# Gate chunks written out by quarters, and two blocks of experts taken out of the sorted lists, in a two-layer kernel on one core

## The chip, the cores and the metric

The kernel runs on one core of one Trainium2 chip. The metric is the time of one execution on the device, in microseconds (us). TensorE (PE) multiplies, VectorE (DVE) and ScalarE (ACT) do elementwise work, GpSimd (POOL) issues the indirect gathers, and SyncE (SP) issues plain loads. ACT also issues DMAs: its stores sit in the same in-order stream as its arithmetic.

## The reference

256 tokens of width 2048 go through two layers in float32. The part that matters here is the expert mixture at the end of the first layer: 16384 experts, 8 heads, 16 experts chosen for each head and token.

```python
q = (xt @ w_pq).reshape(T, PEER_HEADS, 2, PEER_HALF)
s1 = einsum('thd,hkd->thk', q[:, :, 0], sub_k1); s2 = einsum('thd,hkd->thk', q[:, :, 1], sub_k2)
v1, i1 = top_k(s1, 16); v2, i2 = top_k(s2, 16)
cand = (v1[..., :, None] + v2[..., None, :]).reshape(T, 8, 256)
cidx = (i1[..., :, None] * 128 + i2[..., None, :]).reshape(T, 8, 256)
sc, sel = top_k(cand, 16); eidx = take_along_axis(cidx, sel, -1); gates = softmax(sc)
act = gelu(einsum('cd,ced->ce', xc, u_emb[ic]))          # ic, gc: experts and gates of a token
out = einsum('ce,ced->cd', gc * act, v_emb[ic])
```

## The kernel before

**Precision.** Each weight tile is split into a high and a low part (`whi` on ACT, line 123; `wlo` on DVE, line 124), and `mm3` makes three matmuls of 128 x 512 from them (lines 134 to 136). A weight tile `raw` of 128 x 2048 comes by one DMA of 1 MB; `halves` makes two `whi` and two `wlo` of 128 x 1024 from it. There are 3 buffers of `raw` and 4 each of `whi` and `wlo`. One `whi` feeds 12 matmuls.

**The expert mixture.** It has two phases. In the U phase (loop over `n` in 32), PE multiplies all 16384 rows of `u_emb` by the tokens, ACT applies gelu (`act`, line 783), PE transposes (`tp`, line 790), ACT copies (`actT`, line 792) and ACT issues two stores into the DRAM table `AG` (line 794). Below that stream, at low priority, a second stream routes the tokens: top 16, then the gate matrix, then lists of the experts in use.

**Gate chunks.** The dense gate matrix (16384 experts x 256 tokens) is built in four chunks of 64 tokens. For each token PE multiplies two one-hot matrices (`sc`, line 667), ACT copies one half (`gh`, line 672), and DVE adds the other into `gsb` (line 673), a single buffer of 128 x 128 x 64. At the end of a chunk ACT issues two stores of `gsb` to `AG`, 2 MB each, in runs of 256 bytes (line 676), and DVE takes the maximum over the chunk's tokens in one instruction (lines 678 and 681).

**Lists and the V phase.** From those maxima the kernel sorts the experts into blocks of 128: `NA` blocks used by both halves of the tokens, `NB` by the first half alone, `NC` by the second. In the V phase POOL gathers, for each block, 128 rows of `v_emb` (into `raw` or `vraw`, line 130) and their gates and activations from `AG` (`vag`, line 130); `gated` multiplies these (`vh`, `vhh`, `vhl`) and `vblock` adds the block's product into eight PSUM banks: 24 matmuls for an `A` block, 12 for the others. If experts did not fit into the lists, a loop over all 128 blocks (`more > 0`) would finish them.

**Order.** The framework's scheduler lays out one static in-order instruction list for each engine from priorities and a timeline of its own. `prompt` lifts a few instructions of the routing stream to the U phase's priority.

Of the kernel before, what the change touches and what calls it, by code (L numbers as in the profile page):

```python
# [12 lines left out]
F32 = mybir.dt.float32  # L13
# [5 lines left out]
ALU = mybir.AluOpType  # L19
AX = mybir.AxisListType  # L20

P = 128
# [24 lines left out]
NR = _o  # L47


NA, NB, NC = 42, 29, 30  # L50
CAPA, CAP0, CAP1 = NA * 128, (NA + NB) * 128, (NA + NB + NC) * 128
NL = NA + NB + NC
NOWHERE = 127 * 128


@with_exitstack
def tile_kernel(ctx: ExitStack, tc: tile.TileContext, A, out):
    nc = tc.nc
    V, S, G, TE = nc.vector, nc.scalar, nc.gpsimd, nc.tensor

    def pool(name, bufs=1, space=None, stack=ctx):
        kw = {"space": space} if space is not None else {}
        return stack.enter_context(tc.tile_pool(name=name, bufs=bufs, **kw))
# [8 lines left out]
    def bank(name="bk"):  # L72
        tg, nb = {"lin": ("lin", 3), "tp": ("tp", 2), "sc": ("sc", 2), "z": ("sc", 2)}.get(name, ("x", 1))
        return pp.tile([P, 512], F32, tag=tg, name=name, bufs=nb)
# [29 lines left out]
    def wtile(src, step=2048, rows=None, raw=None):  # L104


        if raw is None:
            raw = wp.tile([P, 2048], F32, tag="raw", name="raw", bufs=3)
        if rows is not None:
            gather(raw, src, rows)  # L110
        else:
            for c in range(0, 2048, step):
                nc.sync.dma_start(raw[:, c:c + step], src[:, c:c + step])
        return halves(raw, min(step, 1024))

    def halves(raw, step):
        hi, lo = [], []
        for e in range(2):
            h = wp.tile([P, 1024], F32R, tag="whi", name="whi", bufs=WB)
            l = wp.tile([P, 1024], F32R, tag="wlo", name="wlo", bufs=WB)  # L120
            for c in range(0, 1024, step):
                r, q = raw[:, e * 1024 + c:e * 1024 + c + step], slice(c, c + step)
                S.activation(h[:, q], r, AF.Copy)  # L123
                V.tensor_sub(l[:, q], r, h[:, q].bitcast(F32))  # L124
            hi += [h[:, 0:512], h[:, 512:1024]]
            lo += [l[:, 0:512], l[:, 512:1024]]
        return hi, lo

    def gather(dst, src, rows):
        G.indirect_dma_start(out=dst, out_offset=None, in_=src,  # L130
                             in_offset=bass.IndirectOffsetOnAxis(ap=rows, axis=0))

    def mm3(ps, xh, xl, wh, wl, start, stop):
        TE.matmul(ps, lhsT=xh, rhs=wh, start=start, stop=False)  # L134
        TE.matmul(ps, lhsT=xh, rhs=wl, start=False, stop=False)  # L135
        TE.matmul(ps, lhsT=xl, rhs=wh, start=False, stop=stop)  # L136
# [224 lines left out]
    for c in range(2):  # L361
# [7 lines left out]
        for j in range(0, 4, 2):  # L369
# [9 lines left out]
            for jj in range(2):  # L379
                xh, xl = yl(4 * c + j + jj)  # L380
                split(y[:, jj, :], xh, xl, vcol("g_lru", 4 * c + j + jj))
                for tt in range(2):
# [4 lines left out]
                        axis=AX.X, op=ALU.add)  # L387
# [84 lines left out]
    for c in range(2):  # L472
        ps = linear(WIN, 5 + c, xt, range(4))
        qsb = []
        for tt in range(2):
            q = ap_.tile([P, 8, 64], F32, tag="qsb", name="qsb")
# [49 lines left out]
    AG = dp.tile([129 * P, 512], F32, tag="ag", name="ag")  # L526
    AGv = AG.rearrange("(i p) (e a t) -> p i e a t", p=P, e=2, a=2)
# [22 lines left out]
    for n in range(4):  # L550
        ps = linear(A["w_pq"], n, x1t, range(4))
        qs = []
        for tt in range(2):
            q = rq.tile([P, 512], F32, tag="rq", name="rq", bufs=2)
# [22 lines left out]
    @contextmanager  # L577
    def prompt():

        low[0] = tc.cur_priority  # L580
        tc.cur_priority = low0
        yield
        tc.cur_priority = low[0]
# [9 lines left out]
    for tt in range(2):  # L593
# [23 lines left out]
        for half, op, c in ((0, ALU.logical_shift_right, 4), (1, ALU.bitwise_and, 15)):  # L617
# [5 lines left out]
            for h in range(8):  # L623
# [4 lines left out]
                                op=ALU.mult)  # L628
# [15 lines left out]
    gp = pool("gates", 1, stack=r3p)  # L644


    used = rp.tile([P, 2, P], F32, tag="used", name="used")
# [3 lines left out]
    for c in range(4):  # L651
        gsb = gp.tile([P, P, 64], F32, tag="gsb", name="gsb", bufs=1)
        for t0 in range(0, 64, 4):
            t = 64 * c + t0
            io = iota.unsqueeze(1).to_broadcast([P, 4, P])
            oh = gp.tile([P, 4, P], F32R, tag="oh2", name="oh2", bufs=2)
            V.tensor_tensor(oh, io, i2T[:, t:t + 4].unsqueeze(2).to_broadcast([P, 4, P]), op=ALU.is_equal)
            o1 = gp.tile([P, 4, P], F32, tag="oh1", name="oh1", bufs=2)
            V.tensor_tensor(o1, io, i1T[:, t:t + 4].unsqueeze(2).to_broadcast([P, 4, P]), op=ALU.is_equal)
            og = gp.tile([P, 4, 2, P], F32R, tag="og", name="og", bufs=2)  # L660
            V.tensor_tensor(og[:, :, 1, :], o1, gT[:, t:t + 4].unsqueeze(2).to_broadcast([P, 4, P]), op=ALU.mult)
            for k0 in range(0, 4, 2):
                ps = bank("sc")
                for k in range(k0, k0 + 2):
                    with prompt():
                        S.activation(og[:, k, 0, :], o1[:, k, :], AF.Copy, scale=gTh[:, t + k:t + k + 1])
                        TE.matmul(ps[:, (k - k0) * T:(k - k0 + 1) * T], lhsT=oh[:, k, :],
                                  rhs=og[:, k].rearrange("p a b -> p (a b)"), start=True, stop=True)
                pv = ps.rearrange("p (k m i) -> p m i k", k=2, m=2)
                gh = gp.tile([P, P, 2], F32, tag="gh", name="gh", bufs=2)  # L670
                with prompt():
                    S.activation(gh, pv[:, 0], AF.Copy)
                    V.tensor_tensor(gsb[:, :, t0 + k0:t0 + k0 + 2], gh, pv[:, 1], op=ALU.add)
        h, t0 = c // 2, c % 2 * 64
        for e in range(0, P, 64):
            S.dma_start(AGv[:, 1 + e:65 + e, h, 1, t0:t0 + 64], gsb[:, e:e + 64, :])
        if t0 == 0:
            V.tensor_reduce(used[:, h, :], gsb, axis=AX.X, op=ALU.max)
        else:
            um = gp.tile([P, P], F32, tag="um", name="um")  # L680
            V.tensor_reduce(um, gsb, axis=AX.X, op=ALU.max)
            V.tensor_tensor(used[:, h, :], used[:, h, :], um, op=ALU.max)
    r3p.close()

# [12 lines left out]
    def kt_(name, n=1, dt=F32, bufs=1):  # L697
        return kp.tile([P, n, P], dt, tag=name, name=name, bufs=bufs)

    V.tensor_scalar(used, used, 0.0, None, op0=ALU.is_gt)  # L700
    m3 = kt_("m3", 3)
    V.tensor_tensor(m3[:, 0, :], used[:, 0, :], used[:, 1, :], op=ALU.mult)
    V.tensor_tensor(m3[:, 1:3, :], used, m3[:, 0:1, :].to_broadcast([P, 2, P]), op=ALU.subtract)
# [17 lines left out]
    for i, cap in enumerate((CAPA, CAP0, CAP1)):  # L721
        V.scalar_tensor_tensor(m3[:, i, :], rk[:, i, :], float(cap), m3[:, i, :], op0=ALU.is_lt, op1=ALU.mult)
    V.scalar_tensor_tensor(rk, rk, float(NOWHERE), m3, op0=ALU.subtract, op1=ALU.mult)
    place = kt_("place")
    V.tensor_tensor(place[:, 0, :], rk[:, 0, :], rk[:, 1, :], op=ALU.add)
    V.scalar_tensor_tensor(place[:, 0, :], rk[:, 2, :], float(NOWHERE), place[:, 0, :], op0=ALU.add, op1=ALU.add)
    pli, ti = kt_("pli", 1, I32), kt_("ti", 2, I32)
# [73 lines left out]
    vp = pool("vph", 2, stack=v1)  # L801
# [15 lines left out]
    def tiles_of(b):  # L817
        return (0, 1) if b < NA else (0,) if b < NA + NB else (1,)

    def gated(ag, n):  # L820

        h = vp.tile([P, 4, P], F32, tag="vh", name="vh", bufs=1)[:, 0:n]
        av = ag[:, 0:n * 256].rearrange("p (n a t) -> p n a t", a=2, t=P)
        V.tensor_tensor(h, av[:, :, 0], av[:, :, 1], op=ALU.mult)
        hh = vp.tile([P, 4, P], F32R, tag="vhh", name="vhh", bufs=4)[:, 0:n]
        S.activation(hh, h, AF.Copy)
        hl = vp.tile([P, 4, P], F32R, tag="vhl", name="vhl", bufs=4)[:, 0:n]
        V.tensor_tensor(hl, h, hh.bitcast(F32), op=ALU.subtract)
        return hh, hl

    got = {}
# [24 lines left out]
    def vblock(b, vh, vl, cs, stop=False):  # L856
        for c in cs:
            for tt in tiles_of(b):
                hh, hl = got[b][tt]
                mm3(acc[c][tt], hh, hl, vh[c], vl[c], fresh[tt], stop)  # L860
        for tt in tiles_of(b):
            fresh[tt] = False

    last = []
    for i, b in enumerate(order):
# [6 lines left out]
        vh, vl = wtile(VE, rows=idv[:, b:b + 1], raw=raw)  # L872
# [6 lines left out]
    with tc.If(more > 0):  # L879
        with tc.For_i(0, P, 1) as k:  # L880
            ag = vp.tile([P, 1024], F32, tag="vag", name="vag", bufs=3)
# [6 lines left out]
            hh, hl = gated(ag, 2)  # L888
            raw = wp.tile([P, 2048], F32, tag="raw", name="raw", bufs=3)
            nc.sync.dma_start(raw, VE[bass.ds(k * P, P), :])  # L890
            for c in range(4):
                r = raw[:, c * 512:(c + 1) * 512]
                vh = vp.tile([P, 512], F32R, tag="fh", name="fh", bufs=1)
                S.activation(vh, r, AF.Copy)
                vl = vp.tile([P, 512], F32R, tag="fl", name="fl", bufs=1)
                V.tensor_sub(vl, r, vh.bitcast(F32))
                for tt in range(2):
# [5 lines left out]
                    op=ALU.mult)  # L903
    ssp, ssq = small([P, 2, 4], "ssx"), small([P, 2, 4], "ssx")
    y1t = St(stp, 16, "y1t")
    for c in range(4):
        for i, (b, vh, vl) in enumerate(last):
            vblock(b, vh, vl, (c,), i == 1)
        resid(c, acc[c], None)
        tsplit(lambda tt, j: xs[:, tt, j * P:(j + 1) * P], y1t, 4 * c, 4, lambda j: gfm[:, j:j + 1])  # L910
# [95 lines left out]
    for h0 in (0, 4):  # L1006
        for tt in range(2):
            s = mq.tile([P, 4, T], F32, tag="s2", name="s2", bufs=2)
            for j in range(2):
# [3 lines left out]
                for hh in range(2):  # L1013
                    h = h0 + 2 * j + hh
# [80 lines left out]
    for h0 in (0, 4):  # L1095
        for tt in range(2):
# [4 lines left out]
            for e in range(2):  # L1101
                ps = bank("sc")
                b = slice(64 * e, 64 * e + 64)
                for j in range(2):
                    h = h0 + 2 * j + e
# [172 lines left out]
```

## Time and profile before

| | |
|---|---|
| median of 3 runs | 3051.96 us (3048.44 to 3052.6) |
| the profiled execution, its own time | 3049.11 us |
| its span from first to last instruction | 3047.3 us |
| PE busy | 2970.9 us, 97% |
| DVE / ACT / POOL busy | 66% / 52% / 9% |
| mean granted TensorE clock | 0.990 |
| U phase and routing | about 450 to 1259 us |
| four chunk ends | at 697.5, 828.9, 960.1 and 1087.1 us |
| V phase | about 1271 to 1667 us |

PE is busy nearly throughout, so what a change can win or lose shows as PE idle time, as the number of PE's matmuls, or as matmuls at the lower clock.

### The profile page before, as it was taken

To read this page: it belongs to the slowest core of one execution; us is meant where nothing else is said; L and a number is where in the kernel's file an instruction comes from. 1 tells how busy PE (TensorE), PEld (TensorE's weight loads), DVE (VectorE), ACT (ScalarE), POOL (GpSimd) and SP (SyncE) were. 2 spreads that over 40 slices of the span, in tenths; PEclk is the share of its full clock that TensorE was granted. 3 is DMA by queue.
4 is the path that set the end of the run, shared out by engine and by line. 5 is a ranking of instruction groups with operands and counts; after the bars stand their busy time and mean duration, and the time that the engine had idled before them with its cause. 6 is when DMAs were issued, how large, how long until landed. Compare 5 with 4: busy or idle time off the path is not lost. (4 is left out here: it accounts for less than half of the span.)

```text
span 3047.3 us, 36250 instructions
## 1 busy us (share of the span) xinstructions
PE 2970.9 (97%) x13729; PEld 2443.6 (80%) x13729; DVE 2002.0 (66%) x2944; ACT 1576.9 (52%) x2221; POOL 271.0 (9%) x232
## 2 busy tenths in 40 slices
PE   9999999998988999899999999999999999999999
PEld 7887888887877778678887788778888888888887
DVE  6885789877766769467777756664655454445454
ACT  6754545565655645455565555544444444344443
POOL 0000000000000000477662000000000000000000
PEclk9999999999999999999999999999999999999999
DMA  6442546656567575688886454554655555555554
GB/s 231 155 174 98 180 166 210 215 196 219 189 205 217 181 232 184 226 327 325 333 322 250 173 183 169 205 179 169 242 193 187 194 185 188 193 193 194 190 190 159
DMA packets 197168, 626.26 MB, mean 206 GB/s; under 512 B 82688, under 2 KB 116096, under 8 KB 129664
## 3 DMA queue, kind: packets, MB, share of 16 engines
q1 hardware_dynamic: 73728, 460.55, 42.8%
q0 software_dynamic: 20784, 124.79, 11.1%
q10 hardware_dynamic: 102480, 38.58, 4.8%
q8 instruction: 108, 1.77, 0.2%
q14 instruction: 68, 0.56, 0.1%
HBM read 583.77 MB, written 40.11 MB: 205 GB/s over the span
## 5 line engine op out<-in xcount | busy, mean ns | idle before, releaser
L124 DVE TENSOR_TENSOR wlo<-raw,whi 128x1024 fp32r<-128x1024 f32 (+1 forms) x972 | 1181.4, 1221 | 772.5 <-ACT whi L123 759.8
L123 ACT ACTIVATE whi<-raw 128x1024 fp32r<-128x1024 f32 (+1 forms) x972 | 1023.4, 1057 | 1087.0 <-PE lin L136 901.6
L134 PE MATMUL lin<-whi,x1th 128*128 128x512 f32 x1152 | 451.5, 399 | 25.4 <-ACT whi L123 25.4
L135 PE MATMUL lin<-wlo,x1th 128*128 128x512 f32 x1152 | 457.9, 397 | 6.2 <-DVE wlo L124 6.2
L136 PE MATMUL lin<-whi,x1tl 128*128 128x512 f32 x1152 | 457.1, 397 | 0.0
L134 PEld LDWEIGHTS lin<-whi,x1th 128*128 128x128 f32 x1152 | 219.6, 191 | 70.0 <-ACT whi L123 27.7
L136 PE MATMUL lin<-whi,x3tl 128*128 128x512 f32 x704 | 274.9, 391 | 0.0
L135 PE MATMUL lin<-wlo,x3th 128*128 128x512 f32 x704 | 274.2, 389 | 0.0
L134 PE MATMUL lin<-whi,x3th 128*128 128x512 f32 x704 | 269.5, 390 | 0.0
L135 PEld LDWEIGHTS lin<-wlo,x1th 128*128 128x128 f32 x1152 | 220.4, 191 | 51.3 <-DVE wlo L124 8.5
L136 PEld LDWEIGHTS lin<-whi,x1tl 128*128 128x128 f32 x1152 | 220.1, 191 | 43.5
L135 PE MATMUL lin<-wlo,y1th 128*128 128x512 f32 x512 | 200.7, 393 | 0.8 <-DVE wlo L124 0.8
L134 PE MATMUL lin<-whi,y1th 128*128 128x512 f32 x512 | 199.4, 395 | 1.7 <-ACT y1th L159 1.2
L136 PE MATMUL lin<-whi,y1tl 128*128 128x512 f32 x512 | 198.5, 393 | 0.8 <-DVE y1tl L160 0.8
L135 PEld LDWEIGHTS lin<-wlo,x3th 128*128 128x128 f32 x704 | 132.2, 188 | 27.3
L136 PEld LDWEIGHTS lin<-whi,x3tl 128*128 128x128 f32 x704 | 132.2, 188 | 27.1
L134 PEld LDWEIGHTS lin<-whi,x3th 128*128 128x128 f32 x704 | 132.2, 188 | 26.9
L130 POOL DMA_INDIRECT vag<-ag,idg x102 | 134.2, 1315 | 53.7 <-issue 26.5
L136 PE MATMUL lin<-whi,at 128*128 128x512 f32 x352 | 137.2, 390 | 0.0
L135 PE MATMUL lin<-wlo,at 128*128 128x512 f32 x352 | 137.0, 389 | 0.0
L134 PE MATMUL lin<-whi,at 128*128 128x512 f32 x352 | 135.5, 389 | 0.0
L134 PEld LDWEIGHTS lin<-whi,y1th 128*128 128x128 f32 x512 | 96.2, 188 | 22.4 <-ACT y1th L159 1.8
(440 smaller groups left out, 4750.1 us busy)
## 6 DMA issues: line engine op xcount, KB each, us to landing
raw<-in_u_dram SPq DMA_DIRECT2D x128, 1024.0 KB, 4.8
raw<-in_w_in_dram SPq DMA_DIRECT2D x91, 1024.0 KB, 4.8
raw<-in_w_gu_dram SPq DMA_DIRECT2D x88, 1024.0 KB, 4.8
raw<-in_w_dn_dram SPq DMA_DIRECT2D x44, 1024.0 KB, 4.7
raw<-in_w_out_dram SPq DMA_DIRECT2D x16, 1024.0 KB, 4.8
raw<-in_w_pq_dram SPq DMA_DIRECT2D x16, 1024.0 KB, 4.8
ag<-actT ACTq DMA_DIRECT2D x64, 256.0 KB, 3.0
ag<-gsb ACTq DMA_DIRECT2D x8, 2048.0 KB, 15.5
```

The lines of the kernel that those rows point to most:

```text
L123: S.activation(h[:, q], r, AF.Copy)
L124: V.tensor_sub(l[:, q], r, h[:, q].bitcast(F32))
L130: G.indirect_dma_start(out=dst, out_offset=None, in_=src, in_offset=bass.IndirectOffsetOnAxis(ap=rows, axis=0))
L134: TE.matmul(ps, lhsT=xh, rhs=wh, start=start, stop=False)
L135: TE.matmul(ps, lhsT=xh, rhs=wl, start=False, stop=False)
L136: TE.matmul(ps, lhsT=xl, rhs=wh, start=False, stop=stop)
```

## The change

Each chunk's last addition, its stores and its maximum are cut into four pieces of 32 experts: four additions (line 683 after), four stores of 1 MB (line 684) and four maxima (line 685). The number of 256-byte runs stays the same. Besides, `NB` and `NC` go down by one each, the first two blocks of 128 experts are marked as not in use for the lists (line 708), and the V phase starts with these two whole blocks, for both halves of the tokens: their `vag` and `v_emb` rows come by plain loads from SP, not by gathers.

```diff
-NA, NB, NC = 42, 29, 30
+NA, NB, NC = 42, 28, 29
+ND = 2
...
+                last = t0 + k0 == 62
                 with prompt():
                     S.activation(gh, pv[:, 0], AF.Copy)
-                    V.tensor_tensor(gsb[:, :, t0 + k0:t0 + k0 + 2], gh, pv[:, 1], op=ALU.add)
+                    if not last:
+                        V.tensor_tensor(gsb[:, :, t0 + k0:t0 + k0 + 2], gh, pv[:, 1], op=ALU.add)
         h, t0 = c // 2, c % 2 * 64
-        for e in range(0, P, 64):
-            S.dma_start(AGv[:, 1 + e:65 + e, h, 1, t0:t0 + 64], gsb[:, e:e + 64, :])
+        um = gp.tile([P, P], F32, tag="um", name="um")
+        for e in range(0, P, 32):
+            q = slice(e, e + 32)
+            V.tensor_tensor(gsb[:, q, 62:64], gh[:, q], pv[:, 1, q], op=ALU.add)
+            S.dma_start(AGv[:, 1 + e:33 + e, h, 1, t0:t0 + 64], gsb[:, q, :])
+            V.tensor_reduce(um[:, q], gsb[:, q, :], axis=AX.X, op=ALU.max)
         if t0 == 0:
-            V.tensor_reduce(used[:, h, :], gsb, axis=AX.X, op=ALU.max)
+            V.tensor_copy(used[:, h, :], um)
         else:
-            um = gp.tile([P, P], F32, tag="um", name="um")
-            V.tensor_reduce(um, gsb, axis=AX.X, op=ALU.max)
             V.tensor_tensor(used[:, h, :], used[:, h, :], um, op=ALU.max)
...
     V.tensor_scalar(used, used, 0.0, None, op0=ALU.is_gt)
+    V.memset(used[:, :, 0:ND], 0.0)
...
+    ag = vp.tile([P, 1024], F32, tag="vag", name="vag", bufs=3)
+    for k in range(ND):
+        nc.sync.dma_start(ag[:, k * 512:(k + 1) * 512], AG[(k + 1) * P:(k + 2) * P, :])
+    hh, hl = gated(ag, 2 * ND)
+    for k in range(ND):
+        got[-1 - k] = [(hh[:, 2 * k + tt], hl[:, 2 * k + tt]) for tt in range(2)]
+        vh, vl = wtile(A["v"][k])
+        vblock(-1 - k, vh, vl, range(4))
```

The scheduler lays the rest out anew. Three places follow, as the built programs list them; the numbers behind the names are buffers, which differ between the programs.

ACT at the end of the second chunk, before: the stores of `gsb` stand on either side of two stores of `actT`, and a `whi` follows each.

```order
L676 DMA ag_2894<-gsb_4469 128x64x64
L794 DMA ag_2894<-actT_8349 128x4x128 x2
L123 ACTIVATE whi_8470<-raw_8468 128x1024
L676 DMA ag_2894<-gsb_4469 128x64x64
L123 ACTIVATE whi_8474<-raw_8468 128x1024
L672 ACTIVATE gh_4847<-sc_4842 128x256
L666 ACTIVATE og_4876<-oh1_4874,gTh_2910 128x128 x4
L123 ACTIVATE whi_8525<-raw_8523 128x1024
```

ACT at the same place after the change:

```order
L125 ACTIVATE whi_8562<-raw_8560 128x1024
L684 DMA ag_2894<-gsb_4479 128x32x64 x4
L125 ACTIVATE whi_8566<-raw_8560 128x1024
L675 ACTIVATE gh_4865<-sc_4860 128x256
L668 ACTIVATE og_4894<-oh1_4892,gTh_2910 128x128 x4
L125 ACTIVATE whi_8596<-raw_8594 128x1024
L791 ACTIVATE act_8539<-lin_8401,r1_2876 128x512
L791 ACTIVATE act_8541<-lin_8402,r1_2876 128x512
```

The four stores now stand one behind the other, and the two gelu instructions `act_8539` and `act_8541` of a finished U tile stand behind them.

PE at the same place before: a matmul of `whi_8525` stands early, among those of `whi_8440`.

```order
L134 MATMUL lin_8364<-whi_8440,x1th_2496 128x512
L134 MATMUL lin_8365<-whi_8440,x1th_2496 128x512
L134 MATMUL lin_8521<-whi_8525,x1th_2494 128x512
L135 MATMUL lin_8364<-wlo_8441,x1th_2496 128x512
L136 MATMUL lin_8364<-whi_8440,x1tl_2497 128x512
```

PE at the same place after the change:

```order
L138 MATMUL lin_8402<-whi_8511,x1tl_2497 128x512
L136 MATMUL lin_8558<-whi_8562,x1th_2494 128x512
L798 MATMUL tp_8544<-ident_73,act_8539 128x128
L798 MATMUL tp_8550<-ident_73,act_8539 128x128
L136 MATMUL lin_8559<-whi_8562,x1th_2494 128x512
L798 MATMUL tp_8544<-ident_73,act_8541 128x128
```

Instead of a matmul of a later `whi`, transposes of `act_8539` now stand there, ahead of nearly all matmuls of `whi_8562`.

ACT at the start of the V phase, before: the last `actT` of the U phase goes out right behind its copies.

```order
L783 ACTIVATE act_10857<-lin_10719,r1_2876 128x512
L783 ACTIVATE act_10859<-lin_10720,r1_2876 128x512
L123 ACTIVATE whi_10953<-vraw_10947 128x1024
L792 ACTIVATE actT_10861<-tp_10862 128x512
L792 ACTIVATE actT_10861<-tp_10868 128x512
L794 DMA ag_2894<-actT_10861 128x4x128 x2
```

ACT at the same place after the change:

```order
L791 ACTIVATE act_10894<-lin_10756,r1_2876 128x512
L791 ACTIVATE act_10896<-lin_10757,r1_2876 128x512
L125 ACTIVATE whi_10980<-raw_10974 128x1024
L800 ACTIVATE actT_10898<-tp_10899 128x512
L800 ACTIVATE actT_10898<-tp_10905 128x512
L125 ACTIVATE whi_11030<-raw_11028 128x1024
L802 DMA ag_2894<-actT_10898 128x4x128 x2
```

A `whi` of the first gathered block now stands ahead of the last store. On PE, 14 matmuls of the two whole blocks stand ahead of the last transposes, 7 among them and 27 behind them.

POOL from the first gather of gates on, before:

```order
L130 DMA vag_10894<-ag_2894,idg_2899 128x256 x4
L130 DMA vag_10905<-ag_2894,idg_2899 128x512 x2
L130 DMA vag_10936<-ag_2894,idg_2899 128x256 x4
L130 DMA vag_11003<-ag_2894,idg_2899 128x256
L130 DMA vag_11067<-ag_2894,idg_2899 128x512 x2
L130 DMA vag_11210<-ag_2894,idg_2899 128x512 x2
L130 DMA raw_11132<-in_v_dram,idv_2898 128x2048
```

POOL from the first gather of gates on, after the change:

```order
L132 DMA vag_11008<-ag_2894,idg_2899 128x256 x4
L132 DMA vag_11019<-ag_2894,idg_2899 128x512 x2
L132 DMA vag_11050<-ag_2894,idg_2899 128x256 x4
L132 DMA raw_11190<-in_v_dram,idv_2898 128x2048
L132 DMA vraw_11212<-in_v_dram,idv_2898 128x2048
L132 DMA vag_11117<-ag_2894,idg_2899 128x256
L132 DMA vag_11181<-ag_2894,idg_2899 128x512 x2
L132 DMA vag_11302<-ag_2894,idg_2899 128x512 x2
L132 DMA raw_11246<-in_v_dram,idv_2898 128x2048
```

Two gathers of `v_emb` move ahead of five gathers of gates. Counted on, the gather whose block starts at the 168th matmul behind the first gathered one is the 29th from here before and the 31st after.

## Rows read from the trace of the kernel before

**Rows 1.** The page: busy time of PE, share of the span, instructions.

```profile
PE 2970.9 (97%) x13729; PEld 2443.6 (80%) x13729; DVE 2002.0 (66%) x2944; ACT 1576.9 (52%) x2221; POOL 271.0 (9%) x232
```

**Rows 2.** PE's timeline: matmuls at the higher clock, 0.227 us apart.

```profile
1254.81 0.39 PE L134 MATMUL lin<-whi,x1th 128*128 128x512 f32 x1
1255.03 0.39 PE L135 MATMUL lin<-wlo,x1th 128*128 128x512 f32 x1
```

**Rows 3.** Stretches: width, busy us (PE, PEld, DVE, ACT, POOL), clock, DMA share, GB/s.

```profile
704.00:714.00 10.00, 4.99 (x15) 3.64 (x14) 8.77 (x8) 4.39 (x8) 0.00 (x0) 0.83 0.95 212
727.00:738.00 11.00, 7.48 (x28) 5.59 (x27) 9.12 (x16) 7.30 (x16) 0.00 (x0) 0.84 0.17 50
835.00:850.00 15.00, 7.45 (x21) 5.61 (x20) 9.66 (x9) 5.22 (x9) 0.00 (x0) 0.66 1.04 289
967.00:990.00 23.00, 14.47 (x53) 10.87 (x52) 10.56 (x11) 6.41 (x11) 0.00 (x0) 0.85 0.90 246
1094.00:1106.00 12.00, 6.72 (x18) 5.02 (x17) 6.64 (x6) 3.50 (x4) 0.00 (x0) 0.72 1.05 241
1311.00:1318.00 7.00, 4.51 (x18) 2.77 (x17) 4.06 (x5) 4.47 (x5) 5.30 (x5) 1.00 1.00 415
```

**Rows 4.** Timeline from the U phase to the V phase.

```profile
1256.62 0.39 PE L136 MATMUL lin<-whi,x1tl 128*128 128x512 f32 x1
...
1259.69 0.94 ACTq L794 DMA_DIRECT2D ag<-actT  x2
...
1263.23 0.95 POOL L130 DMA_INDIRECT vag<-ag,idg  x1 [2.08 <-DMA ag<-actT]
...
1271.34 0.80 PE L134 MATMUL tp<-whi,vhh 128*128 128x512 f32 x1 [12.67 <-ACT vhh L826]
```

**Rows 5.** Waits of 690 to 1110 us: who for whom, total, times, longest.

```profile
ACT whi L123 <- issue: 40.4, 4, 10.7
...
PE lin L134 <- ACT whi L123: 25.4, 6, 7.6
```

**Rows 6.** ACT's timeline at the chunk ends: start, length, instruction.

```profile
697.54 0.38 ACTq L676 DMA_DIRECT2D ag<-gsb  x1
697.95 9.98 ACTq L676 DMA_DIRECT2D ag<-gsb  x1
...
828.86 0.38 ACTq L676 DMA_DIRECT2D ag<-gsb  x1
829.28 9.66 ACTq L794 DMA_DIRECT2D ag<-actT  x1
...
960.07 9.37 ACTq L676 DMA_DIRECT2D ag<-gsb  x2
...
973.03 10.98 ACTq L794 DMA_DIRECT2D ag<-actT  x2
...
1087.12 11.12 ACTq L676 DMA_DIRECT2D ag<-gsb  x2
```

**Rows 7.** PE's timeline: the first matmuls after the stalls at the chunk ends.

```profile
710.03 0.69 PE L134 MATMUL lin<-whi,x1th 128*128 128x512 f32 x1 [5.01 <-ACT whi L123]
...
844.07 0.80 PE L134 MATMUL lin<-whi,x1th 128*128 128x512 f32 x1 [7.55 <-ACT whi L123]
...
1100.35 0.79 PE L134 MATMUL lin<-whi,x1th 128*128 128x512 f32 x1 [5.28 <-ACT whi L123]
```

**Rows 8.** DVE's timeline at the first chunk end: the maximum.

```profile
698.03 8.68 DVE L678 TENSOR_REDUCE used<-gsb 128x128 f32<-128x8192 f32 x1
```

**Rows 9.** POOL's and ACT's timeline where the V phase stalls again.

```profile
1306.57 1.46 POOL L130 DMA_INDIRECT raw<-in_v_dram,idv  x1 [0.30 <-issue]
...
1312.82 1.06 ACT L123 ACTIVATE whi<-raw 128x1024 fp32r<-128x1024 f32 x1 [5.90 <-DMA raw<-in_v_dram,idv]
```

## The prediction

> **What bounds the kernel now.** I read the page first. PE is busy 97% of the span [rows 1], so time can only come from three things: PE idle, matmuls added or removed, and matmuls at the lower clock. At the higher clock two matmuls start 0.227 us apart [rows 2].
>
> Then I cut the span into stretches and looked for idle PE. Around the change there are two places. At the ends of the four gate chunks PE is idle for 5.0, 7.55, 8.5 and 5.3 us (width less PE's busy time in the first, third, fourth and fifth stretch) [rows 3], 26.4 us together. Between the phases U and V it stands still for 12.67 us [rows 4].
>
> The table of waits says who is late at the chunk ends: PE waits for `whi` on ACT, and ACT waits in its turn for "issue", 40.4 us in four pieces, that is for nothing the table knows [rows 5]. ACT's timeline shows what it is. The first 2 MB store of a chunk takes 0.38 us to issue, but the next DMA on ACT, whatever its size, takes about 10: the second store 9.98 us, or a 256 KB store of `actT` 9.66 us [rows 6]. From the first store's issue to the end of the hold it is 10.39, 10.08, 9.37 and 11.12 us, a mean of 10.2. ACT is in order, so no `whi` is made meanwhile, and PE runs dry some 7.5 us into the hold: 1st chunk 710.03 - 5.01 - 697.54 = 7.5; 2nd 844.07 - 7.55 - 828.86 = 7.7; 4th 1100.35 - 5.28 - 1087.12 = 8.0 [rows 6, 7].
>
> A held issue thus waits until the store ahead of it has been worked off: 2 MB in 10.2 us is 205 GB/s, and in those stretches the DMA engines stand at a share of 0.9 to 1.05 and move 212 to 289 GB/s [rows 3]. The third chunk confirms it. A second store accepted at 969.4 holds an `actT` store until 984.0 [rows 6], since loads run beside it by then.
>
> [...]
>
> **The change, part by part.**
>
> *Quarters at the chunk ends.* The runs of 256 bytes stay as many, so the whole store takes as long, but ACT is freed only when the last store of a chunk is accepted. Before, that is when the first half is worked off. With four stores in a row it is when three quarters are. Two quarters are the 10.2 us above; the third, 1 MB at the 212 GB/s of the first stretch, takes 4.9 us. The hold becomes 15.2 us instead of 10.2. No row shows a 1 MB store behind another in such runs, so both ends are kept: at the least nothing (0.4 us an issue), at the most 11.12/2 = 5.6 us a quarter, a hold of 17. I take 15.2, since the same hold appeared all four times and followed the bytes, not the issuing instruction.
>
> Chunk by chunk, with PE dry at 7.5 us:
>
> - First: ACT's list behind the hold is as before, two `whi` (2.1 us from ACT's release at 707.93 to PE at 710.03). PE resumes at 15.2 + 2.1, idle 9.8 instead of 5.0: +4.8.
> - Second: PE comes to transposes of `act_8539`, which ACT makes only behind the four stores, a `whi`, a `gh`, four `og` and another `whi`; before, PE waited there for a `whi` behind about the same work (it resumed 4.4 us after ACT was free). With the second gelu, 15.2 + 4.2 + 0.6 - 7.7 = 12.3 instead of 7.55: +4.7.
> - Third: ACT's order is first quarter, two `actT` stores, second quarter, a `whi`, then the last two; the small stores add about 1 us to the hold, and PE waits for a `whi` that comes 3.8 us behind it. 16.2 + 3.8 - 7.6 = 12.4 instead of 8.5: +3.9. The 10.98 us that the `actT` store cost before falls away; it was part of the 8.5.
> - Fourth: PE's matmuls of `whi_10009` and `whi_10013` lie in the hold, and the latter's `wlo` waits for the maxima on DVE. Idle of about 3.3 and 3.6 us instead of 5.3: +1.6.
>
> Together +15.0. The maxima cost nothing by themselves: 8.68 us in one piece [rows 8] or about 9 in four, which stand one behind the other in DVE's order and end inside the hold. If the hold were gone, they would stop `wlo` for those 9 us and PE for 1 or 2. The smaller additions cost 0.4 us of DVE, under the same cover. Some 30 us behind each of the first three ends there is a second gap, as at 727 to 738 (11.0 - 7.5 = 3.5 us) [rows 3], where several one-hot steps stand ahead of a `whi`. After the change the first is better interleaved, the second worse; I count -1, with 3 us either way. Each stall is followed by a few us at the lower clock (0.66 to 0.85 in these stretches) [rows 3]; the number of stalls hardly changes, so neither does this.
>
> *Two whole blocks.* They bring 2 x 24 matmuls; one `B` and one `C` block less save 2 x 12. That is +24 x 0.227 = +5.45 us of PE. What they hide: the last U matmul starts at 1256.62, so PE is free at T = 1256.85, and the first gathered matmul starts at T + 14.5 [rows 4]. Now 14 matmuls (3.2 us) and then 7 more (1.6) stand ahead of or among the last transposes, and a `whi` (about 1.1 us, and it waits for 3 matmuls behind the transposes) ahead of the store. The last `actT` store goes out at about T + 7.8 instead of T + 2.8. From that store to the first gathered matmul it is 1271.34 - 1259.69 = 11.65 us, through landing, four gathers and `gated` [rows 4]; nothing of that changes. The first gathered matmul moves to T + 19.5, 5.0 later, and 24 x 0.227 = 5.45 us fewer remain behind it: -0.4. The whole blocks end at T + 11.8, so a stall of 7.7 us stays, and the clock falls as before. The loads on SP cost nothing: they follow the last U tiles in the same three buffers, hidden under some 8 us of prepared weights.
>
> *Gathers.* Behind the first gate gather POOL is the slow one: PE is idle 2.5 us at 1311 to 1318 (width less busy) [rows 3], where ACT waits for a `v_emb` gather issued at 1306.57 [rows 9]. That is the 29th gather counted from 1263.23, 43.3/28 = 1.55 us each. In the new order the block that PE reaches at the same point (168 matmuls) is the 31st gather, two more, and the next is the 34th where PE has moved 16 matmuls (3.6 us): 3.1 + 0.6 = +3.7 us. Bounds are 0, if POOL's order catches up elsewhere, and 7.
>
> *Lists.* 99 instead of 101 columns save tenths of a microsecond beside other work. Routing the reference's inputs on paper gives 5045 experts for both halves, 3535 and 3436 for one, without the first 256; the places are 42 x 128 + 28 x 128 = 8960 for the first two kinds and 3712 for the last. Nothing is left over, so the loop at the end stays empty.
>
> **Sum.** 15.0 - 1 - 0.4 + 3.7 = +17.3 us. On the profiled execution's own 3049.1 that gives 3066.4; I say 3066. That execution lies 2.9 us below the median of the runs, inside their spread of 4.2. A difference under 0.2% (6.1 us) can't be told from none in this kernel.
>
> **Rivals.**
>
> 1. *The hold goes with the bytes, but the queue takes some descriptors ahead* (same). Then each quarter holds 3 to 4 us, not 5. The three larger terms shrink by 1 us for each us of total hold and the fourth by about a third; at 3.3 us a quarter (10.2 in all) the chunk ends cost what they cost before, and the time is 3049 + 2 = 3051. For it: the small store of 512 runs behind its equal costs almost nothing (0.94 us for two, the last store of the U phase) [rows 4]. Against it: the `actT` store behind a whole half waited as long as another half would [rows 6]. Chance 0.15.
> 2. *Four stores are accepted without a hold* (faster). The place is the chunk ends; the 26.4 us of idle go, and about 8 us of matmuls at the lower clock with them; 2 stay lost to the maxima, and 2.3 us come from the whole blocks, gathers and later gaps: 3049 - 34 + 2 + 2 = 3019. It decides for faster from a hold below some 2.7 us a quarter on. Against it stand all four holds [rows 5, 6]. Chance 0.16, for all values between that point and no hold at all.
> 3. *The third quarter is worked off faster, since ACT, held longer, starts fewer other transfers.* At the 246 GB/s of the third end, instead of 212, it takes 4.3 us, which is 0.6 less a hold: 3066 - 2 = 3064. The share of 0.95 at the first end says that little is free [rows 3]. It lies in the likeliest case's own range. Perfetto Trace Analysis in the Trainium skill, section DMA Optimizations, would have the split start part of the transfer sooner, if DMA engines are idle. By the row just named they aren't.
> 4. *Holds of 5.6 us and stalls in the V phase at their upper bound*: 3066 + 6 + 3 = 3075 or more. Chance 0.07 beyond that.
>
> **How the numbers follow.** The case as summed, 3058 to 3075, has 0.62, rival 3 with it; the others have 0.15, 0.16 and 0.07. Slower is 0.62 + 0.07 = 0.69, same 0.15, faster 0.16. The range of 8 in 10 takes in the first rival with 9 us below it, a part of the second, and reaches to where the fourth begins: 3042 to 3076. The likeliest case's own range is 3058 to 3075.
>
> **What would show it.** At each chunk end the second, third and fourth `gsb` stores should take 4.5 to 5.5 us each to issue, ACT's wait for "issue" should be about 60 us, and PE should be idle about 10, 12, 12 and 7 us. Between U and V there should be one stall of 7 to 8 us, with the last `actT` store some 8 us behind the last U matmul, and a stall of 5 to 7 us about 45 us into the V phase. The prediction is wrong if the second store is issued in 0.4 us, or if ACT's holds still end at 10 us.

## The result and the profile after

The changed kernel takes 3074.32 us (median of 6 runs, 3071.42 to 3077.29) against 3050.57 before (6 runs): 23.8 us more, a ratio of 1.0077 (1.0064 to 1.009). The forecast was slower, 3066 us, 3042 to 3076: the result lies 8 us above the point and 1.7 us inside the upper end. The profiled execution took 3077.29 us; 28 us lie between it and that of before, and its own times below are read against [rows 1 to 9].

The page of the profile has PE at the same share, with 24 matmuls more (13753 against 13729) [rows 1]:

```profile
PE 2982.5 (97%) x13753; PEld 2451.8 (80%) x13753; DVE 2002.9 (65%) x2969; ACT 1580.2 (51%) x2220; POOL 266.3 (9%) x227
```

ACT's timeline at the four chunk ends (start, length, instruction) stands against [rows 6]:

```profile
697.23 0.38 ACTq L684 DMA_DIRECT2D ag<-gsb  x1
697.64 14.97 ACTq L684 DMA_DIRECT2D ag<-gsb  x3
...
838.14 16.16 ACTq L684 DMA_DIRECT2D ag<-gsb  x4
...
973.33 0.38 ACTq L684 DMA_DIRECT2D ag<-gsb  x1
973.75 4.06 ACTq L802 DMA_DIRECT2D ag<-actT  x1
...
979.73 12.48 ACTq L684 DMA_DIRECT2D ag<-gsb  x2
...
1112.10 4.04 ACTq L684 DMA_DIRECT2D ag<-gsb  x1
1116.17 10.88 ACTq L684 DMA_DIRECT2D ag<-gsb  x2
```

The first store is issued in 0.38 us, and three more take 14.97: from the first issue to the release it is 15.38 us, at the second end 16.16, where it was 10.39 and 10.08. ACT's wait for "issue" is 60.9 us instead of 40.4 [rows 5] in the table of waits:

```profile
ACT whi L125 <- issue: 60.9, 6, 15.2
```

PE's timeline shows what this costs (in brackets the idle time before the matmul, and who ended it), against [rows 7] for the chunk ends and [rows 4, 9] for the V phase:

```profile
714.72 0.80 PE L136 MATMUL lin<-whi,x1th 128*128 128x512 f32 x1 [9.80 <-ACT whi L125]
858.47 0.69 PE L798 MATMUL tp<-ident,act 128*128 128x128 f32 x2 [11.73 <-ACT act L791]
995.75 0.80 PE L136 MATMUL lin<-whi,x1th 128*128 128x512 f32 x1 [14.58 <-ACT whi L125]
1128.26 1.22 PE L136 MATMUL lin<-whi,x1th 128*128 128x512 f32 x2 [3.76 <-ACT whi L125]
1146.71 0.94 PE L136 MATMUL lin<-whi,x1th 128*128 128x512 f32 x2 [2.98 <-ACT whi L125]
1295.21 0.80 PE L136 MATMUL tp<-whi,vhh 128*128 128x512 f32 x1 [9.51 <-ACT vhh L834]
1339.12 0.73 PE L136 MATMUL tp<-whi,vhh 128*128 128x512 f32 x2 [2.67 <-ACT whi L125]
1344.50 0.50 PE L136 MATMUL tp<-whi,vhh 128*128 128x512 f32 x1 [1.12 <-ACT whi L125]
1596.21 0.50 PE L136 MATMUL tp<-whi,vhh 128*128 128x512 f32 x1 [2.20 <-ACT whi L125]
```

The stops at the four ends are 9.8, 11.7, 14.6 and 6.7 us. At the second end PE waits for `act`, as forecast, where it waited for a `whi`. The stop between U and V is 9.5 us instead of 12.67. In the V phase there are three stops of more than 1 us, 6.0 us together, and the last, at 1596, stands where the kernel before had none.

ACT's and POOL's timelines between U and V, against [rows 4]:

```profile
1280.38 1.38 ACTq L802 DMA_DIRECT2D ag<-actT  x2
...
1286.43 1.77 POOL L132 DMA_INDIRECT vag<-ag,idg  x1 [8.41 <-DMA ag<-actT]
```

From the last `actT` store to the first gather of gates it is 6.05 us, before 3.54. To the first gathered matmul, at 1295.21, it is 14.8 us, before 11.65.

Three stretches of the two profiled executions share out the 28 us. The last U matmul starts 16.9 us later (1273.49 against 1256.62). From there to the first matmul behind the V phase (at 1694.20, before at 1669.35) it is 420.7 us against 412.7, 8.0 more. The rest to the end of the span is 1381.3 against 1378.0. These last 3.3 us aren't the change: over all thirteen profiled executions, those of the next section among them, the rest is close to 1378 us (before, e3, e5, e8, e9), close to 1381 (after, e1, e2, e4, e6, e7, e10) or between (e11, 1379.9), with the change and without it. In e2 the granted clock is 0.92 and 0.91 in two stretches of 20 us there (1677 to 1698, 1709 to 1729), where in the kernel before it is 1.00 behind the same stops.

### The profile page after: what moved, and what is told of

Same layout as the page of the kernel before. It is cut to its first block, busy times and chain, and to the rows that moved or that the text cites. A ratio compares the mean times of both kernels' runs of the same rounds, so it can differ in the third digit from the quotient of the medians.

```text
span 3075.5 us, 36338 instructions
## 1 busy us (share of the span) xinstructions
PE 2982.5 (97%) x13753; PEld 2451.8 (80%) x13753; DVE 2002.9 (65%) x2969; ACT 1580.2 (51%) x2220; POOL 266.3 (9%) x227
## 6 DMA issues: line engine op xcount, KB each, us to landing
ag<-gsb ACTq DMA_DIRECT2D x16, 1024.0 KB, 11.7
```

## The experiments

Times are compared with the kernel before on the same chip; its medians were 3049.79 to 3050.26 us for the runs that were timed several times. e6, e9 and e10 ran once.

**The parts by themselves (e1, e2).** The first keeps the quarters alone, the second the whole blocks alone.

e1 against the changed kernel (cut at the dots):

```diff
-NA, NB, NC = 42, 28, 29
+NA, NB, NC = 42, 29, 30
...
-    V.memset(used[:, :, 0:ND], 0.0)
...
-    for k in range(ND):
...
-        vblock(-1 - k, vh, vl, range(4))
```

e2 keeps these lines of the changed kernel, and its additions, two 2 MB stores and one maximum a chunk are those of the kernel before.

> Only the gate chunks' quarters; the two whole blocks are left out and the lists have their old lengths. If the loss comes from ACT being held until three quarters of a chunk's store are worked off, the four chunk ends keep about 44 us of idle PE (9.8, 11.7, 14.6, 8.1 us, as in the changed kernel) against 26.4 before, the later gaps 9 against 11, and with a few us of lower clock the time is 3051 + 16 + 3 = 3070 us (3066 to 3073). Rival: the whole blocks and the gathers behind them are the larger part; then this kernel lies at 3058 us or below.

> Only the two whole blocks with the shorter lists; the stores stay in halves. From the parts: 24 more matmuls +5.5, the stop between U and V 13.2 to 9.5 us, -3.7, the gathers' stop in the V phase +4.1: 3051 + 6 = 3057 us (3053 to 3060). Rival: the two parts help or harm each other, so that the blocks alone give 3051 or less, or 3065 or more.

Quarters alone: 3064.02 us, +14.05, ratio 1.0046 (1.0032 to 1.006). Whole blocks alone: 3059.96 us, +10.0, ratio 1.0029 (1.0017 to 1.004). Together that is 24.0, and the whole change was 23.8: the parts add up, within intervals of 9.8 to 18.3 us for the first and 5.2 to 12.2 for the second. e1 is a miss, 2 us below its band: the stops at the chunk ends came about as long as expected (9.8, 12.3, 14.6 and 7.1 us), but in its profiled execution the last U matmul came only 14.4 us later than before, and from there to the first matmul behind the V phase it was 2.5 us less. e2 lies at the upper end of its band. PE's timeline of e2 in the V phase says why:

```profile
1276.72 0.80 PE L136 MATMUL tp<-whi,vhh 128*128 128x512 f32 x1 [8.29 <-ACT vhh L829]
1306.61 0.50 PE L137 MATMUL lin<-wlo,vhh 128*128 128x512 f32 x1 [2.18 <-DVE wlo L126]
1322.14 0.73 PE L136 MATMUL tp<-whi,vhh 128*128 128x512 f32 x2 [1.36 <-ACT whi L125]
1327.79 0.50 PE L136 MATMUL tp<-whi,vhh 128*128 128x512 f32 x1 [1.38 <-ACT whi L125]
1579.13 0.50 PE L136 MATMUL tp<-whi,vhh 128*128 128x512 f32 x1 [2.22 <-ACT whi L125]
```

The stop between U and V went from 12.67 to 8.29 us, but four stops follow, 7.1 us together, where the kernel before had 2.5, all at one place (1311 to 1318) [rows 3]. Stretches of e2 with two of them (columns as in [rows 3]) show the other half:

```profile
1302.00:1312.00 10.00, 7.82 (x28) 5.97 (x27) 6.37 (x6) 2.40 (x3) 8.17 (x7) 0.83 0.59 216
1576.00:1586.00 10.00, 7.78 (x28) 5.94 (x27) 4.72 (x4) 4.18 (x5) 5.80 (x7) 0.83 0.99 405
```

The granted clock is 0.83 of the higher level in both, where it stood at 1.00 around the old stop [rows 3]. At 0.227 us a matmul, 28 take 6.4 us and took 7.8: 1.4 us lost in each. So +5.5 for the matmuls, -4.4 between U and V, +4.6 for stops and +2.9 for the clock make 8.6 us. In the profiled execution it is 8.2 from the last U matmul to the first matmul behind the V phase (420.9 against 412.7); the 10.0 by medians agrees within its interval.

**Who is late in the V phase (e7).** The first ten listed blocks of e2 get their `v_emb` rows by plain loads from SP.

```diff
-        vh, vl = wtile(VE, rows=idv[:, b:b + 1], raw=raw)
+        vh, vl = wtile(A["v"][8 + i], raw=raw) if i < 10 else wtile(VE, rows=idv[:, b:b + 1], raw=raw)
```

> The run of the whole blocks alone (3060 us), but the rows of v_emb of the first ten listed blocks come by plain loads of the same size from SP, without a gather (other rows than the lists name, so the output is not the reference's). Ten gathers fewer on POOL are 13 to 15 us of POOL's time. If POOL's issue is what the stops behind the whole blocks wait for, the stops at about 1307, 1322 and 1328 us (2.2, 1.4 and 1.4 us) and their stretch of lower clock go: 3060 - 5 - 1.5 = 3053.5 us. Rival: the DMA engines are the limit there; the bytes are the same, so the stops stay and the time is 3059 to 3061 us.

Measured 3053.21 us, 6.8 less than e2 (ratio to before 1.0006, 0.9997 to 1.0016). The stops at 1307, 1322 and 1328 are gone, though as many bytes move. The stop between U and V is 2.4 us longer than in e2, and behind it one of more than 2 us is left:

```profile
1280.12 0.80 PE L136 MATMUL tp<-whi,vhh 128*128 128x512 f32 x1 [10.66 <-ACT vhh L829]
...
1575.28 0.50 PE L136 MATMUL tp<-whi,vhh 128*128 128x512 f32 x1 [2.43 <-ACT whi L125]
```

So the early stops wait for POOL's issue and not for the DMA engines. The late one stays. In the changed kernel's trace ACT's `whi` ahead of it waits 4.07 us for a gather of `v_emb` that POOL began at 1587.98, while POOL issued one gather after the other, 0.3 us apart; an experiment on it was not made.

**The same stores from another queue (e3, e4, e5, e11).** e3 and e4 change one word of the kernel before, e5 of e1, and e11 of the changed kernel.

```diff
-            S.dma_start(AGv[...], gsb[...])
+            nc.gpsimd.dma_start(AGv[...], gsb[...])     # e3
+            nc.sync.dma_start(AGv[...], gsb[...])       # e4, e5, e11
```

> The kernel before, but POOL issues the 2 MB stores of the gate chunks. POOL has nothing else to do in the U phase. If ACT's held issue is the whole cause of the four stops, ACT's wait for issue goes from 40.4 us to nearly 0, the 26.4 us of idle PE go to 3 or less, and with 8 us of lower clock the time is about 3051 - 30 = 3021 us. Rival: POOL works off 256-byte runs at the rate of its gathers (128 rows in 0.94 to 1.55 us, so 60 to 100 us for a half); then the next chunk's additions into the one gsb buffer wait some 120 to 200 us, DVE stands behind them, and the time is hundreds of us longer.

> The kernel before, but SP issues the two 2 MB stores of a chunk, one behind the other, with weight loads behind them. If the hold belongs to the queue and goes by bytes, it moves to SP: the second store is held about 10 us, the next load another 10, 20.4 us together, and ACT is not held at all. The weights that lie ahead of PE (up to three raw buffers and two more in whi) last 16 to 22 us less 4.8 for the load, so PE stops for 3 to 9 us a chunk instead of 5 to 8.5: between 3025 and 3055 us. Rival: the hold is ACT's own (its arithmetic waits for a store's data), then SP's loads are not held, and the time is about 3020 us.

> The quarters of the change without the whole blocks, as in the run of the quarters alone, but the four stores are issued by SP. If the quarters cost time only through ACT's hold, the 14 us that they cost on ACT are gone on SP, where the halves took 3025.5 us: 3023 to 3029 us, with ACT waiting for no issue at the chunk ends. SP's loads are then held about 20 us a chunk, as behind the halves (the same bytes). Rival: quarters cost something of their own (more and smaller additions, maxima and DMAs), whoever issues them; then it is 3035 us or more.

> The changed kernel, whole, with one word changed: SP issues the quarters' stores instead of ACT. If the two parts of the change stand by themselves, the whole blocks still cost their 10 us and the quarters nothing: 3027 + 10 = 3037 us (3032 to 3041). Rival: with ACT free, the whole blocks hide the last transposes as they were meant to; then it is 3027 us or less.

From SP it is 3025.53 us, 24.4 less than before (ratio 0.9924, 0.9909 to 0.9939), at the lower end of the band expected; the quarters from SP take 3027.01 (0.9931, 0.9915 to 0.9948), inside theirs: what they cost on ACT is gone. The timelines of SP and ACT in e4 at the first and the third end show the hold on SP's queue:

```profile
696.61 10.48 SPq L676 DMA_DIRECT2D ag<-gsb  x2
708.03 9.76 SPq L113 DMA_DIRECT2D raw<-in_u_dram  x3
...
948.94 9.20 SPq L676 DMA_DIRECT2D ag<-gsb  x2
959.27 10.52 SPq L113 DMA_DIRECT2D raw<-in_u_dram  x1
...
956.32 1.70 ACTq L794 DMA_DIRECT2D ag<-actT  x2
```

SP's second store and the load behind it are held 8.7 to 11.3 us each at the four ends, so the rival, 3020 us with SP's loads free, falls. Two `actT` stores of ACT, in the middle of SP's hold (948.94 to 958.14), go out in 1.70 us: SP's queue is held, and ACT's is not. Perfetto Trace Analysis in the Trainium skill, section DMA Instruction, HWDGE, says that a descriptor generator shared by two sequencers is locked for one DMA at a time. ACT's 1.70 us within SP's 9.20 do not agree with a lock that lasts as long as a hold. The first stops of PE at the four ends are 2.7, 1.5, 1.3 and 1.6 us, where 3 to 9 were expected; in e4 at the first end:

```profile
706.93 0.50 PE L135 MATMUL lin<-wlo,x1th 128*128 128x512 f32 x1 [2.71 <-DVE wlo L124]
726.00 0.83 PE L667 MATMUL sc<-og,oh 128*128 128x256 f32 x4 [1.72 <-DVE gsb L673]
```

The weights that SP has loaded ahead last through its 20 us; those that ACT has prepared ahead lasted 7.5. What is left is `wlo` behind DVE's maximum (2.71) and the additions that wait for `gsb`, which stopped PE as long in the kernel before.

From POOL it is 3059.43 us, +9.5 (1.0022 to 1.0048): a miss, and neither of the two times expected. ACT is free, but the hold is on POOL too, and the store is done later. Timelines of POOL, DVE and PE in e3 at the second end:

```profile
833.36 2.75 POOL L676 DMA_DIRECT2D ag<-gsb  x1 [118.06 <-DVE gsb L673]
850.87 2.76 POOL L676 DMA_DIRECT2D ag<-gsb  x1 [14.75 <-issue]
...
867.11 0.75 DVE L673 TENSOR_TENSOR gsb<-gh,sc 128x256 f32<-128x256 f32 x2 [17.28 <-DMA ag<-gsb]
...
867.58 1.22 PE L667 MATMUL sc<-og,oh 128*128 128x256 f32 x4 [10.12 <-DVE gsb L673]
```

POOL's second store is held 14.75 us, DVE's next addition waits 17.28 for the single `gsb`, and PE stops for 10.12. The wait moved from ACT to DVE. DMA: Bandwidth & Descriptors in the Trainium skill, in its anatomy of one DMA on the GpSimd path, calls descriptor generation small and says that many descriptors can be emitted before it shows. POOL's stores agree in part: 8192 runs take POOL 2.75 us, but the next store stands still for 12.4 to 15.4 us behind them.

The whole change from SP takes 3031.58 us (0.9923 to 0.9956), 0.4 below the band expected. Against e5 the blocks cost 4.6 us by medians and 10.0 by the profiled executions (3031.76 and 3021.81); e5's runs lie between 3021.81 and 3033.75. From the last U matmul to the first matmul behind the V phase, e11's trace has 418.6 us and e5's 412.9: 5.8 us lie where the blocks act, and the rest of the 10.0 elsewhere.

**What the hold goes by (e6, e10, e9).** One store of 4 MB on ACT, eight of 512 KB, and two of 2 MB in long runs.

```diff
-        for e in range(0, P, 64):
-            S.dma_start(AGv[:, 1 + e:65 + e, h, 1, t0:t0 + 64], gsb[:, e:e + 64, :])
+        for e in range(0, P, 128): ... [:, 1 + e:129 + e, ...], gsb[:, e:e + 128, :]     # e6
+        for e in range(0, P, 16): ... [:, 1 + e:17 + e, ...], gsb[:, e:e + 16, :]        # e10
+            S.dma_start(SCR[:, e * 64:(e + 64) * 64], gsb[:, e:e + 64, :].rearrange("p a b -> p (a b)"))  # e9
```

> The kernel before, with one 4 MB store on ACT a chunk in place of two of 2 MB. If the hold goes by the bytes ahead in ACT's queue and only the next DMA feels it: at the first and the fourth end no DMA of ACT comes for more than 20 us, so neither is held and PE's stops of 5.0 and 5.3 us go (to 2.7 or less, the maximum on DVE); at the second a store of actT stands right behind and is held 20 us, twice as long as before (PE idle about 17 us instead of 7.6); at the third it comes some 4 us behind and is held about 16. One time near 3051 + 4 = 3055 us. Rival: the hold belongs to the instruction (about 10 us for the next DMA whatever its size): then 10 us at the second and the third end, and about 3040 us.

> The kernel before, with eight stores of 512 KB on ACT a chunk in place of two of 2 MB; the additions and the maxima stay whole. If ACT is free when the last store is accepted, that is when seven eighths are worked off, the holds of a chunk come to 7/8 of 20.4 = 17.9 us, against 10.2 for halves and 15.3 for quarters, with some whi between them at the second end. PE is idle about 12 to 14 us at each end, and the time is 3051 + 4 x 6.5 = 3077 us. Rival: a small store is taken ahead while another runs; then the holds come to 12 us or less and the time to 3055 us.

> The kernel before, but the two 2 MB stores of a chunk on ACT go to another table in runs of 16 KB, so 128 runs a store in place of 8192 (the gates in AG stay zero, filled by POOL ahead of the chunks, so the output is not the reference's; only the chunk ends are read, not the time). If the hold goes by the bytes alone, the DMA behind the first store is still held about 10 us (7 at the least). If it goes by the number of runs that must be worked off, it is held 1 us or less, and PE's stops at the four ends go down to what the maximum on DVE leaves, 1 to 3 us each.

ACT's timelines, first of e6 at the first two ends:

```profile
697.05 0.38 ACTq L676 DMA_DIRECT2D ag<-gsb  x1
719.18 6.30 ACTq L794 DMA_DIRECT2D ag<-actT  x2
...
830.02 0.38 ACTq L676 DMA_DIRECT2D ag<-gsb  x1
830.44 20.76 ACTq L794 DMA_DIRECT2D ag<-actT  x1
```

then of e10 at the first:

```profile
699.11 0.38 ACTq L676 DMA_DIRECT2D ag<-gsb  x1
699.51 5.41 ACTq L676 DMA_DIRECT2D ag<-gsb  x2
704.99 14.72 ACTq L676 DMA_DIRECT2D ag<-gsb  x5
```

with, from the same stretch, a load that SP issues beside it and the store of ACT that follows:

```profile
710.57 0.33 SPq L113 DMA_DIRECT2D raw<-in_u_dram  x1
711.93 5.64 ACTq L676 DMA_DIRECT2D ag<-gsb  x1
```

and of e9 at the first and the third, with a row of its DMA issues (count, size, median us from issue to landing):

```profile
711.87 0.35 ACTq L681 DMA_DIRECT2D scr<-gsb  x1
712.41 0.38 ACTq L799 DMA_DIRECT2D ag<-actT  x1
...
956.61 0.83 ACTq L681 DMA_DIRECT2D scr<-gsb  x2
...
scr<-gsb ACTq DMA_DIRECT2D x4, 2048.0 KB, 10.0
```

The hold grows with what stands ahead in the queue: a DMA behind 2 MB waits about 10 us, behind 4 MB 20.76, and ACT is held 20.6 us for eighths (699.11 to 719.71), more than the 17.9 worked out. Had a small store been taken ahead, it would be 12. But the same 2 MB in 128 runs instead of 8192 hold nothing: the next DMA is issued in 0.38 us while the store is still some 10 us from landing, and at the third end both stores of 2 MB go out in 0.83 us, where they took 9.37 [rows 6]. So the price is that of the runs, not of the bytes; e9 also writes to another table, and that alone was not tried. The first store of 2048 runs in e10 held the next DMA between 1.1 and 4.5 us at the four ends.

Nor is it a fixed price for a run. The later stores of e10 take mostly 2.0 to 2.6 us each to issue (1.0 to 3.3 in all), but at each of the four ends the one that follows a load of 1 MB on SP by up to 3 us takes 5.3 to 5.6. So the hold follows how fast the runs ahead are worked off beside other transfers, and not only how many they are.

The time of e6, 3066.38 us in one run, is a miss: 3055 was expected. ACT is not held at the first end until the next `actT` comes at 719. But with SP's loads running on beside, the 4 MB take until 725.5 (28.4 us, not 20.4), the additions wait for `gsb`, and PE's stops there add up to 9.2 us (2.67 + 3.16 + 1.72 + 1.66), no less than before with its second gap (5.01 + 1.72 + 1.73). At the fourth end and behind it they are 5.7 us where 5.28 was, and at the second PE stops for 18.63 us instead of 7.55, about as expected. The eighths' 3079.97 us (one run, beside one of before at 3053.07) are 3 above what was expected; PE's longest stops there are 14.3, 14.3, 5.5 and 15.9 us, so the third end was less and the fourth more than the 12 to 14 expected. e9's time is not compared, but its PE stops at the first three ends for 1.5, 1.5 and 1.3 us behind DVE's maximum, and at the fourth for less than 0.8:

```profile
722.22 0.79 PE L135 MATMUL lin<-wlo,x1th 128*128 128x512 f32 x1 [1.50 <-DVE wlo L124]
```

**A faster version (e8).** e4, and POOL sums the gates as a chunk goes, in place of DVE's maximum at its end.

```diff
...
-            V.tensor_reduce(um, gsb, axis=AX.X, op=ALU.max)
+        G.tensor_tensor(um, gsb[:, :, 0:8], gsb[:, :, 8:16], op=ALU.add)
+        for w in range(16, 64, 8):
+            G.tensor_tensor(um, um, gsb[:, :, w:w + 8], op=ALU.add)
+        for w in (4, 2, 1):
+            G.tensor_tensor(um[:, :, 0:w], um[:, :, 0:w], um[:, :, w:2 * w], op=ALU.add)
...
```

> The kernel with the halves issued by SP (3025.5 us), and DVE's maximum of 8.7 us a chunk replaced by ten additions on POOL (the gates are not negative, so a sum over zero says the same as a maximum over zero). If PE's first stop at the chunk ends, now 2.7, 2.2, 1.3 and 1.5 us by wlo waiting behind the maximum, comes from DVE alone, these 7 to 8 us and a few at the lower clock go: 3016 us (3013 to 3020). Rival: POOL's additions take longer than the 22 us for which the store keeps the gsb buffer anyway; then the next chunk's additions wait for POOL, DVE stands behind them, and it is 3030 us or more.

3021.28 us, ratio 0.9907 (0.9891 to 0.9924): 28.5 us less than before, but only 4.2 less than e4, of 7 to 8 expected, and 1.3 above its band. The intervals of the two overlap, so that e8 is faster than e4 isn't shown. At the first end one stop of 1.72 us is left of e4's three. At the second and the third end PE's stops behind the additions into `gsb` are longer than in e4 (1.98 and 1.11, 2.29), and at the fourth end a new stop stands. PE's timeline there and the table of waits (690 to 1130 us):

```profile
1100.24 0.74 PE L134 MATMUL lin<-whi,x1th 128*128 128x512 f32 x2 [3.00 <-ACT whi L123]
...
DVE gsb L673 <- DMA ag<-gsb: 27.4, 3, 10.9
```

DVE, freed of the maximum, now waits 27.4 us for the store to release the single `gsb`, where it waited 16.5 in e4.

## Why the prediction was right, point by point

The mechanism was right for the larger part, the quarters: ACT, held longer, starves PE. The blocks were priced too low, and part of the agreement in numbers is luck.

- *The hold is 15.2 us instead of 10.2.* It was 15.38, 16.16, 15.4 at the fourth end in two pieces (1111.62 to 1127.05), and 18.9 at the third (973.33 to 992.21), where a `whi` and two small stores break it up; 16.2 had been said there.
- *+4.8, +4.7, +3.9, +1.6 at the chunk ends, -1 behind them.* By PE's rows it was 9.80 - 5.01 = +4.8, 11.73 - 7.55 = +4.2, 14.58 - 8.5 = +6.1 and 6.74 - 5.28 = +1.5, and some 1 us less in the later gaps. So the third end was mis-sized by 2.2 us, with the hold there. That e1 measured +14.05 against +14.0 is closer than its interval (9.8 to 18.3) can show: its profiled execution loses 14.4 us up to the last U matmul, that of the changed kernel 16.9.
- *The reason, "a held issue thus waits until the store ahead of it has been worked off", by bytes at 205 GB/s*, gave the right number only since every store here has runs of 256 bytes. e9 shows that the runs hold the queue and the bytes alone don't; that they are worked off more slowly beside other transfers, as the prediction had it for the third end, e10 bears out; that the queue is held and not the engine's arithmetic follows from e4.
- *Rivals 1 and 2* (descriptors taken ahead, no hold) fell with the 14.97 us of three stores, and with e10. Where e9 takes the hold away, only the stops by the maximum stay, as rival 2 had it.
- *Whole blocks, -0.4*: +5.5 for matmuls stood; the stop shrank by 4.4 us in e2 (5.0 said), by 3.2 in the changed kernel, to 9.5 us and not to 7.7. The step that failed is "nothing of that changes", said of the way from the last `actT` store to the first gathered matmul: it took 14.8 us, not 11.65. The store itself went out earlier than forecast, 6.7 us behind T and not 7.8. In the changed kernel a gather of `v_emb` that POOL issued at 1277.08 stands ahead of the store, and the DMA engines are almost full from 1279 to 1283; that this delays the landing is likely, but no run tested it.
- *Gathers, +3.7.* The number came out near, partly by luck: the V phase's stops grew by 4.0 us in the changed kernel and by 4.6 in e2. But where one stop of 5 to 7 us was forecast, the changed kernel has 3.8 at that place (2.67 and 1.12), and another 2.2 at 1596 that no term held. With e7, POOL's lateness is shown as the cause of e2's first three.
- *"The number of stalls hardly changes, so neither does" the clock.* That was said of the chunk ends; for stops in the V phase the sum has no term for the clock at all. The new stops there brought stretches at the lower clock: 2.9 us in e2. In the changed kernel PE's busy time in the V phase grew by 7.4 us, of which 24 matmuls are 5.5: 1.9 us for the clock.

From the last U matmul to the end of the V phase the blocks cost 8.0 us in the changed kernel and 8.2 in e2, where the sum had +3.3; up to the last U matmul it is 16.9 where the sum had +14.0. That is 7.6 us more than the sum of 17.3 in the profiled executions; the medians, 23.8, are 6.5 above it.

## What to carry to other kernels

Before cutting a store into pieces, look at what its queue does next: behind a store of many short runs the next DMA of the same queue is held until the runs are worked off, and an engine that also computes stands still with it, longer the more pieces there are. Give such stores to the queue whose work is prepared furthest ahead (here SP, 20 us, against ACT's 7.5), or make the runs longer. When work is put ahead of a chain of gathers, count the engine that issues them at every later point, not at the next stop alone, and price the way from the last store to the first gather anew.

## What the runs showed of the hardware

The hold is on every queue that was tried, behind a 2 MB store of 8192 runs: on ACT 9.4 to 11.1 us from that store's issue to the release [rows 6], on SP 8.7 to 11.3, on POOL 12.4 to 15.4. It does not cross from SP's queue to ACT's (1.70 us for two stores at 956.32). It grows when other transfers run beside it: 512 KB in 2048 runs hold mostly for 2.0 to 2.6 us, and for 5.3 to 5.6 beside a load of 1 MB (e10). In runs of 16 KB the same bytes hold nothing (0.38 us).
